# Expert stage of a mixture-of-experts block: single-buffered activations and a longer row of split weights

## The chip, the cores and the metric

One Trainium2 chip, and one of its cores. The metric is the device time of one execution of the whole kernel, in microseconds (us). The engines are called by their names in the profile: PE (TensorE matmul), DVE (VectorE), ACT (ScalarE), POOL (GpSimd) and SP (SyncE, which here only issues transfers).

## The reference, cut to what matters

The program is one block of a diffusion model on 2048 tokens of 1024 channels, all in fp32: a mixer layer, and then a layer of 16 experts. Only the second one is touched:

```python
def ec_moe(h, w_router, w_gate_e, w_up_e, w_down_e):
    cap = EC_CAPACITY * l // N_EXPERTS                      # 256 tokens for each of 16 experts
    aff = jax.nn.softmax((h @ w_router).astype(jnp.float32), axis=-1)
    top_aff, top_idx = lax.top_k(jnp.swapaxes(aff, 1, 2), cap)
    def per_set(hs, idx, wgt):
        xs = hs[idx]
        a = jax.nn.silu(jnp.einsum('ecd,edf->ecf', xs, w_gate_e)) * jnp.einsum('ecd,edf->ecf', xs, w_up_e)
        y = jnp.einsum('ecf,efd->ecd', a, w_down_e) * wgt[..., None].astype(hs.dtype)
        return jnp.zeros_like(hs).at[idx.reshape(-1)].add(y.reshape(-1, hs.shape[-1]))
```

Each expert picks its own 256 tokens, gathers their rows, multiplies them with three matrices of 1024 x 1024, and the weighted result is added to the rows it came from. A final RMS norm over all rows follows.

## The kernel before, in words

**Three products for one.** Every fp32 factor is split into a high and a low part in the type fp32r, and `mm3` (L252 to L255) adds three matmuls: high x high, low x high, high x low. A weight matrix comes in *units* of 128 x 1024 fp32 (512 KB). The class `Units` (L60) handles each in three steps: SP loads it into a tile `wraw` (L69), ACT copies it to `whi` (L78), and `wlo` = `wraw` - `whi` is made by DVE or POOL (L85). There are three buffers of each of the three tiles. A `wraw` is free for the next load once `wlo` is made; a pair `whi`, `wlo` is free once PE has used it. `c` counts the units used up, `s` those split, `d` those whose load is issued; `ahead(n)` splits up to `n` units as long as `s < c + nsp`, with `nsp` = 3, and keeps `nraw` = 3 loads issued beyond `s`. Who makes `wlo` is set by `low2`, since `LOWS` holds all four remainders: POOL from the top-k part through expert 0, DVE after that; `low` is not read in this stage.

**An expert has 12 items of 2 units.** `Flow.item` (L156) writes one item in this order: its 48 matmuls; the finish of the item before it; one step of every side generator; `ahead`, which here splits two units. Eight items `gate_up` (L1790) make `a` in eight pieces: ACT sigmoid (L1801), two DVE multiplications (L1802, L1803), ACT writes the high part `ah` (L1804) and DVE the low part `al` (L1805). Four items `down` (L1809) multiply `ah`, `al` with the down matrix, and DVE writes `y` (L1825). Before the first `down` the last piece's finish is written by `fl.flush()`; that piece is read by the last eighth of the item's matmuls (`LATE`, L45).

**The next expert is prepared beside it.** `prep(e + 1)` (L1726) is a side generator that starts with expert `e`: DVE writes a one-hot tile `oh` in two steps of eight (L1731), PE turns it into token numbers (L1737, 32 small matmuls), POOL gathers the rows into `xg0`, `xg1` (L1748), PE transposes them (L1766), and ACT and DVE split the result into `xh`, `xl` (L1771, L1772).

**Ahead of expert 0** stands the top-k search of experts 0 and 1 (`topk_first`, L1681): eight rounds, each a DVE count over a tile (L1684), a matmul, and a few tiny DVE instructions on integers (L1672, L1677, L1678, L1666), one after the other. `prep(0)` follows. One `next()` of that chain is one pass of the loop at L1893; in its first pass `un.ahead()` splits three units, their low parts on POOL. The search for experts 2 to 15 (`topk_rest`) has its eight rounds (DVE count at L1714, L1718, matmul at L1719) between the items of expert 0.

**The last six experts** (`LASTK`) carry more side work: rows of the output that are finished are loaded, normed and stored (`norm_row`, L1836), and each expert's result is added to gathered rows, normed and scattered (L1859 to L1888).

Of the kernel before, what the change touches and what calls it, by code (L numbers as in the profile page):

```python
# [11 lines left out]
F32R = mybir.dt.float32r  # L12
BF = mybir.dt.bfloat16
# [7 lines left out]
D = 1024  # L21
# [5 lines left out]
NSC = L // 128  # L27
# [32 lines left out]
class Units:  # L60
    def __init__(self, nc, pool, srcs, nraw, nsp, rset):
        self.nc, self.pool, self.srcs, self.nraw, self.nsp = nc, pool, srcs, nraw, nsp
        self.raw, self.hl, self.rset = {}, {}, rset
        self.d = self.s = self.c = 0
        self.low = self.low2 = nc.vector

    def _dma(self):
        raw = self.pool.tile([128, 1024], F32, name="wraw", bufs=self.nraw)
# [4 lines left out]
    def _split(self):  # L73
        if self.d == self.s:
            self._dma()
        raw = self.raw.pop(self.s)
        hi = self.pool.tile([128, 1024], F32R, name="whi", bufs=self.nsp)
        self.nc.scalar.activation(hi, raw, AF.Copy)  # L78
        if self.s in self.rset:
            lo = None  # L80
            v = lambda t: t.rearrange("p (k c) -> p k c", c=128)[:, :, 96:128]
            self.nc.vector.tensor_sub(v(hi), v(raw), v(hi).bitcast(F32))
        else:
            lo = self.pool.tile([128, 1024], F32R, name="wlo", bufs=self.nsp)
            (self.low2 if self.s % 4 in LOWS else self.low).tensor_sub(lo, raw, hi.bitcast(F32))  # L85
        self.hl[self.s] = (hi, lo)
        self.s += 1

    def loads(self, n=None):
        while self.d < min(len(self.srcs), self.s + self.nraw if n is None else n):  # L90
            self._dma()
# [138 lines left out]
def build(ctx, tc, A, out, dbg=None):  # L230
# [18 lines left out]

    RT, RG = Ring(ps_t, 2), Ring(ps_g, 4)  # L250

# [30 lines left out]
    un = Units(nc, wp, p1_units + p2_units * NBLK + p2_units[8:] + moe_units, 3, 3, rset)  # L282
# [120 lines left out]
    with tc.tile_pool(name="ada", bufs=1, side="right") as ada:  # L403
# [108 lines left out]
        for i in range(4):  # L512
            p = ps_a()
            for j in range(4):
# [24 lines left out]
                if hl and todo:  # L539
                    n = todo.pop(0)  # L540
# [19 lines left out]
    def x_first():  # L560
# [4 lines left out]
        yield  # L565
        for pr, R, bks in ((0, RG, (0, 1, 2, 3)), (1, RT, (0, 1)), (1, RG, (2, 3))):
            *ps, t = yield from R.get(len(bks))
# [21 lines left out]
    def gla_head(b, h, n, kd, qd, rt, vv, full, done=None, past=None, vdone=None):  # L589
        nch, nsc = n // 64, n // 128  # L590
        hs = slice(h * 128, (h + 1) * 128)
        v3 = lambda t: t.rearrange("p (s i) -> p s i", i=128)
        pz, tz = yield from RG.get()
        PE.matmul(pz[:, :n], wd[:, hs], rt[:, :n], start=True, stop=True)
# [6 lines left out]
        V.tensor_scalar(mz[:, :n], pz[:, :n], bd, 0.0, op0=OP.add, op1=OP.min)  # L601
        RG.put(tz)
        S.activation(zt[:, :n], zt[:, :n], AF.Exp, scale=-1.0)
# [58 lines left out]
        if full:  # L662
            pf, pb, tf = yield from RG.get(2)
            for s in range(4):
# [866 lines left out]
    for bi, b in enumerate(order):  # L1531
# [30 lines left out]
        xg = p2.tile([128, 4, D], F32, name="xg")  # L1562
# [26 lines left out]
    mo = moc.enter_context(tc.tile_pool(name="mo", bufs=1))  # L1589
# [7 lines left out]
        return psum.tile([128, 512], F32, name="pT", bufs=3)  # L1597

    RG = Ring(ps_g, 2)
    gt2 = mo.tile([128, D], F32)  # L1600
    fng = mo.tile([128, D], F32)
    brow(gt2, bc_d[0:1, 3072:4096])
# [123 lines left out]
    def prep(e, res):  # L1726
        while e not in ready:
            yield
        oh = mo.tile([128, NSC, 256], BF, name="oh", bufs=2)
        for t in range(NSC):  # L1730
            V.tensor_scalar(oh[:, t], iob, slot[:, e, t:t + 1], None, op0=OP.is_equal)  # L1731
            if t % 8 == 7:
                yield
        pa, tg = yield from RG.get()
        for t in range(NSC):
            for hf in range(2):
                PE.matmul(pa[:, hf * 5:hf * 5 + 5], oh[:, t, hf * 128:(hf + 1) * 128], aux[:, e, t],  # L1737
                          start=t + hf == 0, stop=t + hf == NSC)
        yield
        ax = mo.tile([128, 2, 5], F32, name="ax", bufs=2)  # L1740
        V.tensor_copy(ax.rearrange("p a b -> p (a b)"), pa[:, 0:10])
        RG.put(tg)
        idx, xg = [], []
        for i in range(2):
            ix = mo.tile([128, 1], I32, name=f"ix{i}", bufs=3)
            V.scalar_tensor_tensor(ix, ax[:, i, 0:1], 128.0, ax[:, i, 1:2], op0=OP.mult, op1=OP.add)
            x = mo.tile([128, D], F32R, name=f"xg{i}", bufs=2)
            G.indirect_dma_start(out=x.bitcast(F32), out_offset=None, in_=h2_d[:, :],  # L1748
                                 in_offset=bass.IndirectOffsetOnAxis(ap=ix[:, :1], axis=0))
            idx.append(ix)  # L1750
            xg.append(x)
        wt = mo.tile([128, 2], F32, name="wt", bufs=3)
        V.tensor_add(wt, ax[:, :, 2], ax[:, :, 3])
        V.tensor_add(wt, wt, ax[:, :, 4])
        if e == 0:
            for _ in range(PRE):
                next(rest)
        yield
        yield
        xh = mo.tile([128, KC, 256], F32R, name="xh", bufs=2)  # L1760
        xl = mo.tile([128, KC, 256], F32R, name="xl", bufs=2)
        def trans(p, bk, i):
            for k2 in range(2):
                kc = bk * 2 + k2
                o = (k2 * 2 + i) * 128
                PE.transpose(p[:, o:o + 128].bitcast(F32R), xg[i][:, kc * 128:(kc + 1) * 128], identr)  # L1766

        def evac(p, bk):
            p3 = p.rearrange("p (k t) -> p k t", k=2)
            ks = slice(bk * 2, bk * 2 + 2)  # L1770
            S.activation(xh[:, ks], p3, AF.Copy)  # L1771
            V.tensor_sub(xl[:, ks], p3, xh[:, ks].bitcast(F32))  # L1772

        if e == 0:
            ps = [ps_t(), ps_t(), ps_t(), ps_a()]
            for i in range(2):
                for bk in range(4):
                    trans(ps[bk], bk, i)
            for bk in range(4):
                evac(ps[bk], bk)  # L1780
        else:
            for bk in range(4):
                p = ps_t()
                for i in range(2):
                    trans(p, bk, i)
                yield
                evac(p, bk)
        res[e] = (xh, xl, idx, wt)
# [103 lines left out]
    un.low = un.low2 = G  # L1892
    for n, _ in enumerate(chain(topk_first(), prep(0, res))):  # L1893
        next(keys, None)
        if n == 0:
            un.ahead()
            un.low = V
    for e in range(E):
        special = e >= E - LASTK
        xh, xl, idx, wt = res.pop(e)  # L1900
        ah = mo.tile([128, 8, 256], F32R, name="ah", bufs=2)
        al = mo.tile([128, 8, 256], F32R, name="al", bufs=2)
        if e + 1 < E:
            fl.add(prep(e + 1, res))
        un.low2 = G if e == 0 else V
        if e == 0:
            fl.early.append(rest)
            fl.add(chain(delay(AD), split_aff(slice(HEAD_N, E), E - HEAD_N)))
        acs = []
        if special:  # L1910
            fl.add(acc_gather(idx, acs))
        if e == E - LASTK:
            fl.add(chain(delay(2), staggered([lambda t=t: norm_row(t) for t in range(NSC)], 4)))
        for f in range(8):
            gate_up(f, xh, xl, ah, al)
        y = [mo.tile([128, D], F32, name=f"y{i}", bufs=2) for i in range(2)]

        ss4 = mo.tile([128, 2, 4], F32, name="ss4", bufs=2)

        def fin_cols(j, i, e=e, y=y, acs=acs, ss4=ss4, idx=idx):  # L1920
            cs = slice(j * 256, (j + 1) * 256)
            V.tensor_add(y[i][:, cs], y[i][:, cs], acs[i][:, cs])
            if j < 2 or e < E - 1:
                fl.add(fin_late(j, i, e, y, acs, ss4, cs))
                return
            for _ in fin_late(j, i, e, y, acs, ss4, cs):
                pass
            if j == 3 and e == E - 1:
                for _ in final_row(i, e, y, acs, ss4, idx):
                    pass  # L1930

        def scat(e=e, y=y, idx=idx, special=special, ss4=ss4, acs=acs):
            if special and e < E - 1:
                fl.add(chain(delay(1), staggered([lambda i=i: final_row(i, e, y, acs, ss4, idx) for i in range(2)], 1)))
            elif not special:
                for i in range(2):
                    G.indirect_dma_start(out=x1_d[:, :],
                                         out_offset=bass.IndirectOffsetOnAxis(ap=idx[i][:, :1], axis=0),
                                         in_=y[i], in_offset=None, compute_op=OP.add)
        fl.flush()  # L1940
        for j in range(4):
            down(j, ah, al, y, wt, fin_cols if special else None, scat if j == 3 else None,
                 e == E - 1 and j == 3)
        fl.flush()
        if e == E - 1:
            fl.drain()
# [75 lines left out]
```

## Time and profile before

| | us |
|---|---|
| runs of the kernel, median of 3 | 2662.35 |
| lowest and highest of the 3 | 2653.22 and 2670.72 |
| span of the profiled execution, first to last instruction | 2667.8 |

The profiled execution's own time is not listed apart from its span; its span lies between the median and the highest run. In the span PE is busy for 2517.5 us (94%), DVE for 1881.2, ACT for 1252.5, POOL for 659.1. About 1440 us pass up to the end of the mixer's last product; some 40 us of top-k search and `prep(0)` follow, and the rest of the span belongs to the 16 experts.

### The profile page before, as it was taken

How to read it: one execution, taken by the hardware profiler on the slowest of the kernel's cores; microseconds unless marked ns; L12 is line 12 of the kernel's file. 1: busy time of each engine (PE TensorE's matmuls, PEld its weight loads, DVE VectorE, ACT ScalarE, POOL GpSimd, SP SyncE). 2: the span in 40 equal slices, each digit the busy share in tenths (PEclk: the TensorE clock that was granted, in tenths of full speed). 3: DMA queues.
4: the chain of work that ended last, by engine and by line, in shares of the span. 5: the costliest groups of instructions: out<-in, count | busy, mean ns of one | idle time of the engine just before them, and what ended most of it. 6: DMA issues, size and time to landing. Idle time of an engine off the chain costs nothing. (4 is left out here: it accounts for less than half of the span.)

```text
span 2667.8 us, 44973 instructions
## 1 busy us (share of the span) xinstructions
PE 2517.5 (94%) x17575; PEld 2295.5 (86%) x17575; DVE 1881.2 (71%) x3049; ACT 1252.5 (47%) x2128; POOL 659.1 (25%) x607
## 2 busy tenths in 40 slices
PE   7999999999998989999996899999999999999997
PEld 4878887887887768897886789999999999999997
DVE  6676668478368767767676866666666667778775
ACT  5454444344453345455553334444444445555553
POOL 0032157055225202131312550000000002323222
PEclk9999999999999989999997899999999999999999
DMA  7354356456435766656664356666666667787775
GB/s 259 125 188 164 137 186 220 144 174 213 161 112 170 251 225 221 222 185 225 199 210 139 127 174 212 215 204 209 212 207 214 211 209 251 262 276 258 252 248 183
DMA packets 202141, 537.00 MB, mean 201 GB/s; under 512 B 20871, under 2 KB 60216, under 8 KB 201928
## 3 DMA queue, kind: packets, MB, share of 16 engines
q1 hardware_dynamic: 141224, 408.77, 45.2%
q0 software_dynamic: 18592, 67.64, 8.8%
q10 hardware_dynamic: 42112, 57.72, 6.0%
q8 instruction: 138, 2.26, 0.3%
q14 instruction: 75, 0.61, 0.1%
HBM read 441.76 MB, written 92.29 MB: 200 GB/s over the span
## 5 line engine op out<-in xcount | busy, mean ns | idle before, releaser
L85 DVE TENSOR_TENSOR wlo<-wraw,whi 128x1024 fp32r<-128x1024 f32 x563 | 723.6, 1293 | 414.8 <-ACT whi L78 389.7
L78 ACT ACTIVATE whi<-wraw 128x1024 fp32r<-128x1024 f32 x595 | 623.8, 1055 | 619.7 <-PE pA L254 246.7
L255 PE MATMUL pA<-xh,wlo 128*128 128x256 f32 x2048 | 579.9, 283 | 17.3 <-DVE wlo L85 13.4
L253 PE MATMUL pA<-xh,whi 128*128 128x256 f32 x2048 | 582.1, 284 | 2.1 <-ACT whi L78 2.1
L254 PE MATMUL pA<-xl,whi 128*128 128x256 f32 x2048 | 577.4, 282 | 0.1
L255 PEld LDWEIGHTS pA<-xh,wlo 128*128 128x128 f32 x2048 | 388.0, 189 | 22.0 <-DVE wlo L85 17.4
L253 PEld LDWEIGHTS pA<-xh,whi 128*128 128x128 f32 x2048 | 388.0, 189 | 3.3 <-ACT whi L78 3.1
L254 PEld LDWEIGHTS pA<-xl,whi 128*128 128x128 f32 x2048 | 388.0, 189 | 0.4 <-DVE xl L1772 0.4
L253 PE MATMUL pA<-hh,whi 128*128 128x512 f32 (+1 forms) x912 | 366.4, 402 | 10.9 <-DVE kd L770 3.7
L255 PE MATMUL pA<-hh,wlo 128*128 128x512 f32 (+1 forms) x912 | 359.3, 394 | 0.4 <-DVE wlo L85 0.4
L254 PE MATMUL pA<-hl,whi 128*128 128x512 f32 (+1 forms) x912 | 359.1, 394 | 0.0
L253 PE MATMUL pA<-whi,ah 128*128 128x256 f32 x1024 | 290.3, 284 | 5.0 <-ACT ah L1804 5.0
L254 PE MATMUL pA<-wlo,ah 128*128 128x256 f32 x1024 | 287.4, 281 | 1.8 <-POOL wlo L85 1.1
L255 PE MATMUL pA<-whi,al 128*128 128x256 f32 x1024 | 287.8, 281 | 0.2 <-DVE al L1805 0.2
L253 PEld LDWEIGHTS pA<-hh,whi 128*128 128x128 f32 x912 | 175.4, 192 | 54.2 <-issue 8.9
L255 PEld LDWEIGHTS pA<-hh,wlo 128*128 128x128 f32 x912 | 174.9, 192 | 38.1 <-DVE wlo L85 0.7
L254 PEld LDWEIGHTS pA<-hl,whi 128*128 128x128 f32 x912 | 175.5, 192 | 34.3
L253 PEld LDWEIGHTS pA<-whi,ah 128*128 128x128 f32 x1024 | 193.7, 189 | 5.8 <-ACT ah L1804 5.8
L254 PEld LDWEIGHTS pA<-wlo,ah 128*128 128x128 f32 x1024 | 193.9, 189 | 2.6 <-POOL wlo L85 1.3
L255 PEld LDWEIGHTS pA<-whi,al 128*128 128x128 f32 x1024 | 193.7, 189 | 1.0 <-DVE al L1805 1.0
L1804 ACT ACTIVATE ah<-sg 128x256 fp32r<-128x256 f32 x128 | 53.5, 418 | 275.6 <-DVE sg L1803 275.6
L297 POOL TENSOR_TENSOR rs<-ms,neg_half 128x1 f32<-128x1 f32 (+2 forms) x70 | 54.5, 779 | 509.1 <-DVE ms L295 496.0
(438 smaller groups left out, 4787.7 us busy)
## 6 DMA issues: line engine op xcount, KB each, us to landing
wraw<-win SPq DMA_DIRECT2D x139, 512.0 KB
wraw<-wg SPq DMA_DIRECT2D x128, 512.0 KB
wraw<-wu SPq DMA_DIRECT2D x128, 512.0 KB
wraw<-wdn SPq DMA_DIRECT2D x128, 512.0 KB
wraw<-wout SPq DMA_DIRECT2D x40, 512.0 KB
ar<-ada SPq DMA_DIRECT2D x64, 256.0 KB
gate_d<-stg ACTq DMA_DIRECT2D x64, 256.0 KB
wraw<-wpj SPq DMA_DIRECT2D x32, 512.0 KB
```

Source lines behind the costliest of these rows:

```text
L78: self.nc.scalar.activation(hi, raw, AF.Copy)
L85: (self.low2 if self.s % 4 in LOWS else self.low).tensor_sub(lo, raw, hi.bitcast(F32))
L253: PE.matmul(ps, lh, rh, start=first, stop=False)
L254: PE.matmul(ps, lh, rl, start=False, stop=False)
L255: PE.matmul(ps, ll, rh, start=False, stop=last)
L297: G.tensor_tensor(r[:, :n], ms[:, :n], neg_half[:, :n], op=OP.pow)
L1804: S.activation(ah[:, f], sg, AF.Copy)
```

## The change

Three groups of tiles lose their second buffer: `ah` and `al` (8 KB of each partition each), `xg0` and `xg1` (4 KB each), `oh` (8 KB). The 32 KB hold four more pairs `whi`, `wlo`, which are taken from the stage's own pool `mo`; with the three of the pool `wp` they make seven. `nsp` becomes 7 when the stage begins (`widen`), and units go round through four buffers of the one and three of the other pool. The number of `wraw` buffers stays three. The loop over the search and `prep(0)` splits one unit in each pass, for seven passes, where it split three in the first pass.

```diff
+    def widen(self, pool, n):
+        self.more, self.nm, self.nsp = pool, n, self.nsp + n
+        self.k = 0
+
+    def _out(self, name):
+        if self.more is None:
+            return self.pool.tile([128, 1024], F32R, name=name, bufs=self.nsp)
+        if self.k % self.nsp < self.nm:
+            return self.more.tile([128, 1024], F32R, name=name + "m", bufs=self.nm)
+        return self.pool.tile([128, 1024], F32R, name=name, bufs=self.nsp - self.nm)
...
-        hi = self.pool.tile([128, 1024], F32R, name="whi", bufs=self.nsp)
+        hi = self._out("whi")
...
-            lo = self.pool.tile([128, 1024], F32R, name="wlo", bufs=self.nsp)
+            lo = self._out("wlo")
...
+        if self.more is not None:
+            self.k += 1
...
     RG = Ring(ps_g, 2)
+    un.widen(mo, 4)
...
-        oh = mo.tile([128, NSC, 256], BF, name="oh", bufs=2)
+        oh = mo.tile([128, NSC, 256], BF, name="oh")
...
-            x = mo.tile([128, D], F32R, name=f"xg{i}", bufs=2)
+            x = mo.tile([128, D], F32R, name=f"xg{i}")
...
     for n, _ in enumerate(chain(topk_first(), prep(0, res))):
         next(keys, None)
-        if n == 0:
-            un.ahead()
+        un.ahead(1)
+        if un.s == un.c + un.nsp:
             un.low = V
...
-        ah = mo.tile([128, 8, 256], F32R, name="ah", bufs=2)
-        al = mo.tile([128, 8, 256], F32R, name="al", bufs=2)
+        ah = mo.tile([128, 8, 256], F32R, name="ah")
+        al = mo.tile([128, 8, 256], F32R, name="al")
```

## Rows read from the trace of the kernel before

**Rows 1.** Timeline, PE, one-hot matmuls of three experts: start us, us, engine, line, instruction.
```profile
1657.60 0.96 PE L1737 MATMUL pG<-aux,oh 128*128 128x5 bf16 x32
...
2219.53 0.63 PE L1737 MATMUL pG<-aux,oh 128*128 128x5 bf16 x19
...
2519.23 0.91 PE L1737 MATMUL pG<-aux,oh 128*128 128x5 bf16 x30
```

**Rows 2.** Waits, PE, 1480 to 1600 us: who for whom, us in total, times, longest.
```profile
PE pG L1719 <- DVE mv L1718: 4.7, 2, 2.4
PE pA L255 <- POOL wlo L85: 3.9, 3, 3.0
...
PE pA L255 <- DVE wlo L85: 1.8, 2, 1.3
```

**Rows 3.** Waits, PE, 1600 us to the end.
```profile
PE pA L255 <- DVE wlo L85: 11.6, 13, 2.3
PE pA L253 <- ACT ah L1804: 5.0, 4, 2.1
```

**Rows 4.** Waits, ACT, 2348 to 2425 us (about expert 12).
```profile
ACT whi L78 <- DMA wraw<-wdn: 7.7, 3, 4.5
...
ACT whi L78 <- PE pA L254: 0.5, 1, 0.5
```

**Rows 5.** Waits, DVE, the same stretch, its longest.
```profile
DVE wlo L85 <- ACT whi L78: 11.7, 13, 2.2
```

**Rows 6.** Timeline, ACT then PE, 2401 to 2405 us; in brackets idle before, and what ended it.
```profile
2401.13 1.06 ACT L78 ACTIVATE whi<-wraw 128x1024 fp32r<-128x1024 f32 x1 [2.38 <-DMA wraw<-wdn]
...
2404.44 0.42 ACT L1804 ACTIVATE ah<-sg 128x256 fp32r<-128x256 f32 x1 [0.94 <-DVE sg L1803]
...
2404.91 0.39 PE L253 MATMUL pA<-whi,ah 128*128 128x256 f32 x1 [1.55 <-ACT ah L1804]
```

**Rows 7.** The chain of waits, 2366 to 2445 us, one load: start us, us.
```profile
2394.25 6.78 DMA wraw<-wdn
```

**Rows 8.** Timeline, POOL, DVE and SP, 1445 to 1455 us, search rounds of experts 0 and 1.
```profile
1446.23 6.95 POOL L85 TENSOR_TENSOR wlo<-wraw,whi 128x1024 fp32r<-128x1024 f32 x3 [3.94 <-ACT whi L78]
...
1445.01 0.16 DVE L1677 SCALAR_TENSOR_TENSOR cand<-dg,pj 128x1 int32<-128x1 int32 x1
...
1446.92 1.68 DVE L1677 SCALAR_TENSOR_TENSOR cand<-dg,pj 128x1 int32<-128x1 int32 x1
...
1449.31 1.59 DVE L1666 TENSOR_TENSOR pj<-P,jx 128x1 int32<-128x1 int32 x1
...
1451.04 2.15 DVE L1677 SCALAR_TENSOR_TENSOR cand<-dg,pj 128x1 int32<-128x1 int32 x1
...
1454.94 0.16 DVE L1677 SCALAR_TENSOR_TENSOR cand<-dg,pj 128x1 int32<-128x1 int32 x1
...
1448.61 0.33 SPq L69 DMA_DIRECT2D wraw<-wu  x1
```

**Rows 9.** Timeline, PE and DVE, 1511 to 1519 us, in expert 0.
```profile
1513.36 0.58 PE L255 MATMUL pA<-xh,wlo 128*128 128x256 f32 x1 [3.03 <-POOL wlo L85]
...
1511.38 4.27 DVE L1666 TENSOR_TENSOR pj<-P,jx 128x1 int32<-128x1 int32 x1
...
1518.69 0.17 DVE L1672 SCALAR_TENSOR_TENSOR m<-pG,mk 128x8 f32<-128x8 f32 x1 [1.20 <-PE pG L1719]
```

**Rows 10.** Timeline, ACT, DVE and POOL, 1694 to 1733 us, between two experts.
```profile
1694.81 0.58 ACT L1771 ACTIVATE xh<-pT 128x512 fp32r<-128x512 f32 x1
...
1719.65 0.42 ACT L1804 ACTIVATE ah<-sg 128x256 fp32r<-128x256 f32 x1 [1.81 <-DVE sg L1803]
...
1713.19 0.87 DVE L1825 SCALAR_TENSOR_TENSOR y<-pA,wt,gt 128x256 f32<-128x256 f32 x2
1713.98 1.74 DVE L1731 TENSOR_SCALAR oh<-iob,slot 128x256 bf16<-128x256 bf16 x8
...
1732.99 0.99 POOL L1748 DMA_INDIRECT xg<-h_d,ix  x1 [8.32 <-DVE wt L1754]
```

More of the change, by code (lines that the diff above doesn't have):

```diff
@@ L65, in __init__ @@
         self.low = self.low2 = nc.vector
+        self.more, self.nm = None, 0
+    def widen(self, pool, n):
[7 more added lines that the diff above has]
+        return self.pool.tile([128, 1024], F32R, name=name, bufs=self.nsp - self.nm)
     def _dma(self):
```

## The prediction

> **What bounds the kernel now.** I read the rows in the order of the stage's parts, since each has another limit. First the rhythm of the stage: one expert's one-hot matmuls follow the last expert's by the length of one expert [rows 1]. Between 1657.60 and 2219.53 us lie eight experts, so 70.24 us each; the three waits of PE that lead its list after 1600 us are nearly all in the last part, so in this middle part PE is the bound, and nothing that the change does to weights can make it faster. From 2219.53 to 2519.23 us four experts take 74.93 us each: 4.7 us lost per expert. Second, PE's waits [rows 2, 3]. In experts 0 and 1 they are for the search of experts 2 to 15 (4.7 us), for a low part from POOL (3.9 us) and for one from DVE (1.8 us). After 1600 us they are for `wlo` from DVE (11.6 us in 13 waits) and for `ah` at the turn from gate/up to down (5.0 us in 4). By these sums the last six experts seem to be short of weights in store, and a longer row of split units seems the remedy.
>
> Third, the question that decides: who waits for whom in those experts? Around expert 12 ACT waits 7.7 us for loads of down weights alone, and for PE 0.5 us in all; DVE's list holds only ACT [rows 4, 5]. So there PE is not what sets the pace. ACT and DVE go through their own instructions, in written order, as fast as the loads and their own work let them, and PE follows. The reader is to see this once in one place: ACT's copy at 2401.13 us waited 2.38 us for a load; behind it in ACT's order stands the last piece of `ah`, written at 2404.44 us, and PE had stood 1.55 us for it by 2404.91 us [rows 6]. Between issue and landing of such a load lie 6.78 us [rows 7].
>
> **The change, part by part.** The sum is made against the profiled execution, whose span of 2667.8 us is 5.4 us above the median of the runs shown; I carry the differences over to the median.
>
> *One buffer for `ah`, `al`, `oh`, `xg`.* Costs nothing, as the second buffer is not in use before. At the turn to the next expert the last `y` is evicted at 1713.19 us, so every reader of the old `ah` is done; the first write to the new one comes at 1719.65 us, 6.5 us later [rows 10]. The one-hots of 1713.98 us stand 56 us behind the matmuls that read the ones before (1657.60 us) [rows 1, 10], and the gather of 1732.99 us 38 us behind the evacuation (1694.81 us) of the rows gathered before [rows 10]. What hides it is the order in which the work is written; with that cover gone the wait would stand on ACT, DVE or POOL ahead of the splits.
>
> *Four more splits in the search.* SP gets four more loads there, ACT four more copies (1.06 us each [rows 6]), POOL four more subtractions. ACT's share is covered: the search runs on DVE and PE. SP has nothing urgent behind these loads, and the gather on POOL comes after the search. POOL's share is not covered. Three subtractions run from 1446.23 us for 6.95 us, 2.32 us each. In these 7 us three tiny integer instructions of DVE take 1.68, 1.59 and 2.15 us, where their like takes 0.16 before and after [rows 8]. The search's rounds show the price: from 1445.01 to 1446.92 us 1.91 us, and then 4.12 and 3.90 us (to 1451.04 and 1454.94), so 4.2 us for three, 1.4 us per subtraction. When do the new four run? The load of the fourth unit is issued at 1448.61 us, when the first subtraction gives its buffer back [rows 8]; with 6.78 us for a load [rows 7] and 1.06 us for the copy it can be subtracted from 1456.5 us on, and the others follow at 2.3 us or more. At 1454.94 us the fifth of eight rounds begins, and slots and one-hots follow, so all four fall among DVE work that PE idles for. 4 x 1.4 = +5.6 us. Bounds: 0, if they meet only instructions that POOL doesn't hold up; 9.3 us, if each holds DVE up for its whole length. I take the middle row, since it is the same work in the same loop.
>
> The Trainium skill ("SBUF — State Buffer", "Who interferes with whom") has a rule against this part: VectorE with two inputs from SBUF, or in a two-port mode, and GpSimd share a pair of ports, and the second to come is blocked until the first is through. The trace agrees with the 2.15 us beside 0.16; by the rule at its worst, a whole POOL instruction for each, this term would be the upper bound above.
>
> *Expert 0.* Here POOL still makes the low parts, two for each item as before. A store of four units more takes away PE's 3.9 us of waiting for POOL [rows 2], but PE also runs the search's matmuls between the items, and these wait for DVE. At 1513.36 us PE had stood 3.03 us for a low part; in the same time DVE sat in one integer instruction for 4.27 us, from 1511.38 us, and when it came to the next round it waited only 1.20 us for PE [rows 9]. What PE gains beyond that is waited off at the search. I take -1.2 us; bounds 0 and -3.9.
>
> *Expert 1.* DVE is relieved of the search, PE's 1.8 us of waiting for DVE's low parts goes [rows 2], and 680 us of PE-bound work lie behind it in which ACT and DVE catch up: -1.8 us; bounds 0 and that.
>
> *Experts 2 to 9.* Nothing: PE is the bound.
>
> *The last experts.* With seven pairs PE doesn't wait for `wlo` any more: the 11.6 us [rows 3] go from that line. What is late next is `ah`. The order of ACT's and DVE's instructions is not changed: in each item they still split two units, behind the same loads through the same three `wraw` buffers, and the last piece of `ah` still stands behind the last split of its expert. Since they hardly wait for PE, they reach that piece at the same time as before, and PE, earlier there by what it saved, waits there for as much longer. Once per expert the store is of no use. What can be gained is what ACT and DVE themselves wait for PE: 0.5 us [rows 4] for each of five experts, -2.5 us. Bounds: 0, and -19 us if the saved waits stay saved (below).
>
> Sum: +5.6 - 1.2 - 1.8 - 2.5 = +0.1 us, so 2662 us.
>
> **The rivals.**
> *Faster: the store carries over the turn.* ACT and DVE would have to catch up between a shortage and the next `ah`. For it: the shortages are short (13 waits, the longest 2.3 us), and expert by expert the loss is only 4.7 us. Against it: rows 4 and 5. Price: four experts lose 4 x 4.7 = 18.8 us up to 2519.23 us, and the remaining 1.7 another 8, together 27; the share of `wlo` in the waits for `wlo` and `ah` is 11.6 / 16.6, so 19 us. +5.6 - 1.2 - 1.8 - 19 = -16: 2646 us. Chance 0.22.
>
> *Slower: POOL holds up the search.* Place: the lead-in of expert 0. The price per subtraction is its whole 2.32 us instead of 1.4, since the slots and one-hots are closer packed than the rounds, and nothing comes back in expert 0 or at the end: +9.3 - 1.8 = +7.5, 2670 us. It decides from (1.2 + 1.8 + 2.5) / 4 = 1.4 us per subtraction on: that is just the price measured, so the sign of my sum is open. Chance 0.2.
>
> *Much slower: the single buffers bind.* If each expert's first piece kept PE waiting for its finish (1.81 + 0.42 us [rows 10]), 15 x 2.2 = 33 us: 2695 us. The Trainium skill ("Trainium Kernel Development and Optimization", "Best Practices") asks for double buffers so that transfers overlap compute; no row here shows the second buffer in use. Chance 0.03.
>
> *The store stays empty*, because loads come too slowly to fill it in the search: then the added cost and the gain both shrink, and the time is the forecast's. I count it with the forecast.
>
> **How the numbers follow.** Forecast 0.52, faster 0.22, slower 0.2, single buffers 0.03; 0.03 for what I don't see. The runs before differ by 17 us, so a median of three can be off by several us. The range takes in the faster case at 2646 less 4 and the slower one at 2670 plus 5: 2642 to 2675; the forecast's own is 2656 to 2668. A difference of 1% (26.6 us, about what a measurement of this kernel can tell from no change) needs a time under 2636 or over 2689: 0.07 for the first, the faster case with the expert 0 bound on top; 0.05 for the second, single buffers and the unseen; 0.88 between.
>
> **What would show it.** Right: PE's first `gate_up` of expert 0 begins 4 to 8 us later, with long integer instructions of DVE beside seven POOL subtractions; after 1600 us PE's waits for `wlo` are near zero and those for `ah` rise from 5.0 to 12 us or more; the last experts still take 74 to 75 us each. Wrong: `ah` waits stay at 5 us while `wlo` waits go, and the last experts come near 71 us (faster case); or the search isn't longer, which makes the time about 2657 us; or PE stands at the first items of each expert (single buffers).

## The result and the profile after

The changed kernel takes 2678.95 us (median of 7 runs, 2673.68 to 2682.94), the one before 2663.94 us on the same chip (7 runs): the ratio is 1.0061, with an interval of 1.0043 to 1.008. It is 15 us slower, where 2662 us and no change were forecast, and it lies above the range.

The profiled execution of after has a span of 2671.7 us and is the fastest of its seven, while that of before lies above its median. So the spans differ by only 3.9 us. But the first count of the search, ahead of which the two kernels do the same work, comes 4.9 us earlier in the profile of after (1436.46 against 1441.40 us). From that count to the end it is 1235.2 us for 1226.4: 8.8 us more. I compare stage by stage.

The rhythm, in the timeline of PE in the kernel after (start us, us, instruction; the same three experts as [rows 1]):
```profile
1658.98 0.96 PE L1752 MATMUL pG<-aux,oh 128*128 128x5 bf16 x32
...
2224.78 0.96 PE L1752 MATMUL pG<-aux,oh 128*128 128x5 bf16 x32
...
2525.51 0.96 PE L1752 MATMUL pG<-aux,oh 128*128 128x5 bf16 x32
```
Eight middle experts now take 565.80 us where it was 561.93 us [rows 1]: 70.73 us each for 70.24. The next four take 300.73 us for 299.70, and from there to the end it is 146.2 us for 148.6.

The lead-in, in the timeline of POOL and DVE in the kernel after (in brackets the idle time before, and what ended it), as [rows 8]:
```profile
1441.28 9.38 POOL L97 TENSOR_TENSOR wlom<-wraw,whim 128x1024 fp32r<-128x1024 f32 x4 [3.94 <-ACT whim L90]
1450.62 2.35 POOL L97 TENSOR_TENSOR wlo<-wraw,whi 128x1024 fp32r<-128x1024 f32 x1
1457.02 4.65 POOL L97 TENSOR_TENSOR wlo<-wraw,whi 128x1024 fp32r<-128x1024 f32 x2 [4.05 <-ACT whi L90]
...
1436.46 0.73 DVE L1699 TENSOR_SCALAR_CACHE_REDUCE tjk<-key,jx 128x512 bf16<-128x512 f32 x1
...
1441.99 1.65 DVE L1692 SCALAR_TENSOR_TENSOR cand<-dg,pj 128x1 int32<-128x1 int32 x1
...
1444.35 1.60 DVE L1681 TENSOR_TENSOR pj<-P,jx 128x1 int32<-128x1 int32 x1
...
1446.10 2.15 DVE L1692 SCALAR_TENSOR_TENSOR cand<-dg,pj 128x1 int32<-128x1 int32 x1
...
1448.96 1.72 DVE L1681 TENSOR_TENSOR pj<-P,jx 128x1 int32<-128x1 int32 x1
...
1450.82 2.16 DVE L1692 SCALAR_TENSOR_TENSOR cand<-dg,pj 128x1 int32<-128x1 int32 x1
...
1458.55 0.83 DVE L1693 SCALAR_TENSOR_TENSOR P<-dg,P 128x1 int32<-128x1 int32 x1
...
1460.14 1.58 DVE L1645 TENSOR_TENSOR msk<-aff,t 128x32 bf16<-128x32 f32 x1
...
1476.05 1.89 DVE L1787 TENSOR_TENSOR xl<-pT,xh 128x512 fp32r<-128x512 f32 x3 [5.19 <-ACT xh L1786]
```
Seven subtractions, and beside each of them one small DVE instruction that is held: three `cand`, two `pj`, a `P` and a `msk`, 0.83 to 2.16 us where 0.15 to 0.20 us is usual. Each ends within 0.1 us of the end of its subtraction. Together they take 10.6 us more than usual; the three of before [rows 8] took 5.0 us more. From the first count to the first `xl` it is 39.59 us; before it was 35.42 us (1441.40 to 1476.82). From there to the one-hot matmuls in the third expert (the first of [rows 1]) it is 182.93 us for 180.78.

Waits of PE in the kernel after (who for whom, us in total, times, longest), from 1480 to 1600 us, as [rows 2], and from 1600 us to the end, as [rows 3]:
```profile
PE pG L1734 <- DVE mv L1733: 11.8, 4, 4.4
PE pA L269 <- DVE al L1820: 1.7, 1, 1.7
...
PE pT L1781 <- DMA xg<-h_d,ix: 12.0, 7, 3.3
PE pA L267 <- ACT ah L1819: 6.3, 5, 2.6
```
Not one wait for a weight is left. In experts 0 and 1 PE waits for the search (`mv`) in their place. In the last experts it waits for the gathered rows `xg`, 12.0 us, and for `ah`, 6.3 us: 18.3 us in all, where five kinds of wait (the two of [rows 3] the largest) made 19.8 us before.

One such wait, in the timeline of PE and POOL:
```profile
2469.64 0.33 PE L1781 MATMUL pT<-identr,xg 128*128 128x128 f32 x2 [3.31 <-DMA xg<-h_d,ix]
...
2462.11 1.86 POOL L1763 DMA_INDIRECT xg<-h_d,ix  x1 [0.19 <-issue]
```
PE has the weights and comes to the transposes 3.31 us before the rows that POOL asked for at 2462.11 us are there. The indices for this gather are written by DVE, 8.86 us behind the one-hot matmuls of the same expert (2457.06 against 2448.20 us); before it was 4.94 us (2447.84 against 2442.90).

Waits of ACT in the kernel after, 2273 to 2600 us, those for loads (as in [rows 4], here for all the last experts):
```profile
ACT whim L90 <- DMA wraw<-wg: 18.8, 10, 3.6
ACT whim L90 <- DMA wraw<-wu: 11.0, 5, 3.9
ACT whi L90 <- DMA wraw<-wg: 10.8, 5, 4.0
ACT whi L90 <- DMA wraw<-wu: 5.4, 3, 2.7
ACT whim L90 <- DMA wraw<-wdn: 5.0, 4, 1.6
...
ACT whi L90 <- DMA wraw<-wdn: 4.0, 4, 1.3
```
Together 55.0 us in 31 waits; in the same stretch of before they are 47.1 us in 28. Four more pairs did nothing for the waits that hold ACT's order up.

### The profile page after: what moved, and what is told of

Read it like the earlier page. It is cut to its first block, busy times and chain, and to the rows that moved or that the text cites. A ratio compares the mean times of both kernels' runs of the same rounds, so it can differ in the third digit from the quotient of the medians.

```text
span 2671.7 us, 45172 instructions
## 1 busy us (share of the span) xinstructions
PE 2514.9 (94%) x17575; PEld 2298.7 (86%) x17575; DVE 1885.2 (71%) x3045; ACT 1252.7 (47%) x2128; POOL 675.1 (25%) x611
## 5 line engine op out<-in xcount | busy, mean ns | idle before, releaser
L97 DVE TENSOR_TENSOR wlo<-wraw,whi 128x1024 fp32r<-128x1024 f32 x358 | 461.1, 1293 | 277.2 <-ACT whi L90 264.8
L90 ACT ACTIVATE whi<-wraw 128x1024 fp32r<-128x1024 f32 x375 | 393.8, 1055 | 423.8 <-PE pA L268 226.4
L97 DVE TENSOR_TENSOR wlom<-wraw,whim 128x1024 fp32r<-128x1024 f32 x201 | 257.4, 1287 | 135.2 <-ACT whim L90 131.4
L267 PE MATMUL pA<-xh,whim 128*128 128x256 f32 x1176 | 335.5, 285 | 0.0
L268 PE MATMUL pA<-xl,whim 128*128 128x256 f32 x1176 | 333.0, 283 | 0.1
L269 PE MATMUL pA<-xh,wlom 128*128 128x256 f32 x1176 | 332.8, 283 | 0.0
L90 ACT ACTIVATE whim<-wraw 128x1024 fp32r<-128x1024 f32 x220 | 230.6, 1055 | 191.8 <-PE pA L269 68.6
L267 PE MATMUL pA<-xh,whi 128*128 128x256 f32 x872 | 248.5, 285 | 0.0
L268 PE MATMUL pA<-xl,whi 128*128 128x256 f32 x872 | 246.5, 283 | 0.0
L269 PE MATMUL pA<-xh,wlo 128*128 128x256 f32 x872 | 246.4, 283 | 0.0
```

Source lines behind the costliest of these rows:

```text
L267: PE.matmul(ps, lh, rh, start=first, stop=False)
L268: PE.matmul(ps, lh, rl, start=False, stop=False)
L269: PE.matmul(ps, ll, rh, start=False, stop=last)
```

## The experiments

Each ratio is against runs of the kernel before on the same chip, with its interval; medians of different experiments can come from different chips. "Middle experts" is the mean of eight from the one-hot matmuls of one expert to those eight later, as in [rows 1].

**1. One part alone: the single buffers** (before, with the four `bufs=2` of the diff removed, the freed memory left empty).

> The kernel before with single buffers for ah, al, oh and the gathered rows; three pairs of split weights and the lead-in stay as before, the freed memory is unused. Theory A (single buffers cost nothing; the loss is made of the lead-in, of slower matmuls on the new weight tiles, and of gains that turn into waits elsewhere): ratio 1.000 within 0.003, 70.2 us per expert in the middle part, PE's wait for gathered rows in the last experts under 2 us as before. Rival S (single buffers bind: the gather waits for its one buffer): PE's wait for gathered rows 10 us or more, as in the changed kernel (12.0 us), ratio 1.003 to 1.006.

2663.95 us, ratio 1.0004 (0.9982 to 1.0026), 70.24 us per middle expert. The second buffers were not in use.

**2. The lead-in undone and the pairs filled later:**
```diff
-    un.widen(mo, 4)
...
-        un.ahead(1)
-        if un.s == un.c + un.nsp:
+        if n == 0:
+            un.ahead()
             un.low = V
...
+        if e == 1:
+            un.widen(mo, 4)
```

> The changed kernel, but with the lead-in of before (three pairs split in the search, all by POOL) and the four further pairs added only when expert 1 begins, split by DVE. Their tiles come to lie at the top of the stage's memory. Theory A: the 4 us in the lead-in go, and what experts 0 and 1 lost with them; the middle part is at 70.2 or at 70.8 us per expert according to where the tiles lie; ratio 1.000 to 1.004. Rival L (the lead-in is all of the loss): ratio 1.000 or below. Rival S (single buffers bind): ratio 1.006 as the changed kernel.

2666.68 us, ratio 1.0014 (0.9992 to 1.0037). First count to first `xl` 35.6 us again. But the step from expert 1's one-hots to expert 2's grew to 98.0 us (95.1 in the changed kernel, 93.3 before): filling the store costs there too. And the middle experts took 69.75 us, less than before. The pairs had been allocated later and so stood elsewhere in memory; nothing else in that stage had changed. That was the first sign of what I had missed.

**3. Three pairs only, all in the new memory** (`widen(mo, 3)` with `nsp` = 3, old lead-in).

> The changed kernel with three pairs of split weights instead of seven, and all three in the new memory where the changed kernel has its four; lead-in of before. Theory A, part on placement (matmuls that read the new tiles run slower, 0.55 us per expert with 4 of 7 units there): with all units there 0.9 to 1.0 us per expert, so 71.1 to 71.2 us per expert in the middle part, ratio 1.004 to 1.006. Rival D (the slower pace comes with the number of pairs, or from somewhere else): 70.2 us per expert, ratio 1.000.

2669.59 us, ratio 1.0022 (1.0 to 1.0044), 70.84 us per middle expert, less than the 71.1 us I expected. Number and rotation of the pairs are those of before, and the single buffers cost nothing (experiment 1); only the place is new, and PE is slower.

**4. The same memory for raw weights** (single buffers, three pairs, seven `wraw` tiles):
```diff
+        if self.k % self.nraw < self.nm:
+            raw = self.more.tile([128, 1024], F32, name="wrawm", bufs=self.nm)
+        else:
+            raw = self.pool.tile([128, 1024], F32, name="wraw", bufs=self.nraw - self.nm)
```

> The kernel before with single buffers, and 16 of the 32 KB used for four more tiles of raw weights instead: seven loads under way or landed, three pairs split. Theory A, part on the last experts (ACT and DVE are held up there by loads that are issued only when one of three raw buffers comes free): the last experts fall from 74.9 us towards 71 to 72.5 us each, ACT's waits for weight loads after 2273 us fall below 10 us, ratio 0.991 to 0.996. Rival W (DVE's and ACT's own work in written order is the bound, or the transfers are): 74 to 75 us each, ratio 0.998 to 1.001.

2645.28 us, ratio 0.9929 (0.9907 to 0.9951). The middle experts stay at 70.25 us, and the last steps are 71.0 to 71.9 us where it was 71.4 to 76.8. The longest waits of ACT in this kernel, 2273 to 2600 us, and PE's waits from 1600 us on:
```profile
ACT ah L1817 <- DVE sg L1816: 88.2, 37, 5.9
ACT whi L90 <- PE pA L267: 17.4, 11, 2.0
...
PE pA L267 <- DVE wlo L97: 3.0, 9, 0.8
```
ACT's list holds no more waits for weight loads; its copies wait for PE, and PE's own waits have come down to 3.0 us, so PE is the bound. That settles the last experts: they were held by loads issued too late through three `wraw` buffers.

**5, 6. The place of the pairs, and the lead-in, each alone** (the changed kernel with the four pairs in a pool opened behind `mo`; the changed kernel with `if n == 0: un.ahead(3)` in the lead-in).

> The changed kernel with one difference: its four extra pairs stand at the top of the memory (behind every other tile of the expert stage) instead of at its bottom; seven pairs, the seven low parts on POOL in the lead-in and everything else as changed. Theory (the matmuls' pace depends on where their operands stand): the nine middle experts fall from some 70.75 us each to 69.6 to 70.0, the fifteen in all by 12 to 16 us, so 2663 to 2667 us. Rival (the slower pace comes from seven pairs in rotation or from what the lead-in left behind): 2677 to 2681 us and 70.7 us an expert.

2668.15 us, ratio 1.0024 (1.0008 to 1.004), 69.75 us per middle expert: 10.8 us less by place alone.

> The changed kernel, but only three low parts on POOL in the lead-in, as in the kernel before; the other four units are split in expert 0's first item. Place and number of the pairs as changed. Theory: the first count to the first xl goes back from 39.6 us to 35.5 (4 us less), the burst of four splits in expert 0 gives 0 to 3 us of that back, and the middle experts stay at 70.75: 2675 to 2680 us. Rival (the lead-in on POOL is most of the loss, through what it delays behind it): 2664 to 2668 us.

2680.41 us, ratio 1.0072 (1.0049 to 1.0096). The lead-in is back at 34.7 us (1440.08 to 1474.80), but the step from expert 0's one-hots to expert 1's went from 34.5 to 43.1 us. I had expected 0 to 3 us there. Written all at once into expert 0's first item, the four extra splits cost more (8.6 us) than spread over the lead-in (4.9 us).

**7, 8. Raw tiles and two more pairs; three pairs at the top** (the third experiment with the other pool).

> Single buffers, seven raw-weight tiles (four of them in the freed memory) and five pairs (two of them at the top of memory); three low parts on POOL in the lead-in, the other two splits in expert 0's first item. Theory (the last six experts are held by ScalarE's waits for late loads, more pairs give nothing, the place of the pairs some tenths of a us an expert): the last five steps near 71.5 us as with seven raw tiles alone, 2638 to 2646 us. Rival (pairs are worth something once the loads are early, PE then runs free in the last experts too): under 2636 us.

2639.59 us, ratio 0.9913 (0.9891 to 0.9935), 69.8 us per middle expert. The four steps up to the last one-hots are 69.7, 70.9, 70.4 and 73.6 us: no better than with seven raw tiles and three pairs.

> Three pairs only, all of them at the top of the memory of the expert stage; single buffers, lead-in as before. It is the run with three pairs at the bottom of the new memory (2669.6 us, 70.85 us an expert) with the place alone changed. Theory (place): 69.3 to 69.8 us per middle expert, 2650 to 2660 us. Rival (place among the new tiles is nothing; any tile outside the old pool is slower): 70.8 us an expert and 2668 to 2671 us.

2652.65 us, ratio 0.9967 (0.995 to 0.9984), 69.16 us per middle expert against 70.84 in the third experiment.

**9, 10. All pairs at the top, the six old tiles as raw tiles, with three and four pairs.**

> Three pairs, all at the top of the freed memory, and nine raw-weight tiles: the old three and the six tiles of the old pairs, which are free now. Single buffers, lead-in as before. Theory (the place is worth 1.1 us an expert against the kernel before, early loads some 17 us in the last experts, and the two add): the middle experts at 69.2 us, the last steps 70 to 72 us, 2626 to 2634 us. Rival (the six old tiles as targets of the loads disturb something, or the two gains overlap): 2638 us or more.

2630.46 us, ratio 0.9882 (0.9863 to 0.99), the fastest kernel of this study with the last one below. The two gains add.

> As the run with three pairs and nine raw tiles, with a fourth pair at the top; its first split stands in expert 0's first item. Theory (more pairs are worth nothing once the loads are early, each costs 1 to 2 us to fill at the start): 0 to 3 us above the run with three pairs. Rival (a fourth pair takes the rest of PE's waits in the last experts): 3 to 6 us below it.

2639.32 us, ratio 0.9909 (0.9889 to 0.9929): 9 us worse by the medians (4.4 us by the two profiled spans), more than I expected of a fourth pair. In its profile PE waits 15.3 us for gathered rows in the last experts, where the run with three pairs has 3.7 us.

**11. Seven pairs, but only three ahead in the last experts:**
```diff
-        while n and self.s < len(self.srcs) and self.s < self.c + self.nsp:
+        while n and self.s < len(self.srcs) and self.s < self.c + min(self.nsp, self.cap):
...
+        if e == E - LASTK:
+            un.cap = 3
```

> The changed kernel, but from the first of the last six experts on units are split no further ahead than three, as before; lead-in, buffers and place as changed. Theory (the last experts are set by the order of work on ScalarE and VectorE and their waits for late loads, and how far ahead the splits run only decides which wait shows): TensorE's waits for gathered rows in that stretch fall from 12.0 us to under 3 and waits for wlo come back to some 9 to 12 us, the steps stay at 72 to 78 us, 2675 to 2683 us. Rival (running seven ahead is worth several us there, the gain was only hidden by the slower matmuls): 2685 us or more.

2667.18 us, ratio 1.002 (1.0006 to 1.0034): faster than the changed kernel, which neither theory allowed. PE's waits in this kernel, 2265 us to the end, the longest three:
```profile
PE pA L269 <- DVE wlom L97: 5.3, 7, 1.4
PE pA L269 <- DVE wlo L97: 3.6, 3, 2.1
PE pA L267 <- ACT ah L1819: 3.1, 4, 1.2
```
The waits for gathered rows are gone and weight waits are back, as expected: in experts 12 to 15 DVE writes the indices 4.4 to 5.1 us behind the one-hot matmuls, where it is 6.9 to 8.9 us in the changed kernel. But the medians differ by 11.8 us, of which the two profiles show 4.0 (spans 2667.7 and 2671.7), behind the last one-hots. So running far ahead is of no use there and seems to cost. How much is not settled.

**12. The same three pairs one place lower** (behind `al`).

> The run with three pairs at the top, with the pairs one place lower: directly behind al, 31 KB of each partition below the top place, all tiles of x, ah and al where they were in that run. Theory (what counts is that the pairs stand behind the x and ah tiles and not in front of them): 69.1 to 69.3 us per middle expert, 2650 to 2656 us. Rival (the pace falls evenly with the address, from 70.85 us at 94 KB to 69.16 at 195 KB): 69.6 to 69.8 us per middle expert and 2658 to 2663 us.

2672.77 us, ratio 1.004 (1.0026 to 1.0054), 71.5 us per middle expert: the slowest place of all, and both theories wrong. It is neither "behind x" nor "high". One thing in which the three places, before and after do differ is the start of the pairs against the start of `x`, `xl`, `ah` and `al`, taken modulo 128 bytes of a partition. The compiled programs place `x` at 32 throughout; the pairs stand at 32 here (offset 0), at 64 in the kernel before (32), at 96 at the top (64), and at 0 in the third experiment and the changed kernel's four new pairs (96). The same matmuls at offset 0, in this kernel, PE, 1660 to 2150 us (in the line the count, busy us, mean ns) and in its timeline:
```profile
L267 PE MATMUL pA<-xh,whim 128*128 128x256 f32 x871 | 247.9, 285 | 0.0
...
1720.09 0.28 PE L269 MATMUL pA<-xh,wlom 128*128 128x256 f32 x1
...
1720.69 0.28 PE L268 MATMUL pA<-xl,whim 128*128 128x256 f32 x1
```
and at offset 64, in the kernel with three pairs at the top:
```profile
L267 PE MATMUL pA<-xh,whim 128*128 128x256 f32 x915 | 255.8, 280 | 0.0
...
1720.09 0.28 PE L269 MATMUL pA<-xh,wlom 128*128 128x256 f32 x1
...
1720.66 0.28 PE L268 MATMUL pA<-xl,whim 128*128 128x256 f32 x1
```
Five starts later it is 0.60 us in the one and 0.57 us in the other. Neither line shows a wait. Over all neighbours less than 150 ns apart between 1660 and 2150 us the gate and up matmuls start every 120.0 ns at offset 0, 118.3 ns at 32 (before), 114.9 ns at 64 and 118.4 ns (third experiment) at 96. The down matmuls, where the weights are the 256 columns and `ah` or `al` is the operand of 128 x 128, start every 120.0, 116.9, 117.1 and 120.0 ns: 96 is as slow as 0 for them, while for gate and up it is no slower than 32.

That is where the changed kernel loses, since it has both places side by side. Its down matmuls on the four new pairs (`whim`, `wlom`, offset 96) and on the three old ones (`whi`, `wlo`, offset 32), PE, 1660 to 2150 us:
```profile
L267 PE MATMUL pA<-whim,ah 128*128 128x256 f32 x256 | 72.8, 284 | 0.0
...
L268 PE MATMUL pA<-wlom,ah 128*128 128x256 f32 x256 | 72.1, 282 | 0.0
L267 PE MATMUL pA<-whi,ah 128*128 128x256 f32 x192 | 54.1, 282 | 0.0
...
L268 PE MATMUL pA<-wlo,ah 128*128 128x256 f32 x192 | 53.6, 279 | 0.0
```
Start to start it is 119.9 ns on the new pairs and 117.0 on the old; for gate and up it is 119.0 and 118.3. For four sevenths of an expert's 192 down and 384 gate and up matmuls that makes 0.46 of the 0.48 us that a middle expert lost, and two thirds of it are the down matmuls'.

**13 to 16. The offset alone, by pads of 64 to 96 bytes.** The pads are tiles of 16, 16, 16 + 8 and 24 words, such as
```diff
+        if e == 0:
+            pad = mo.tile([128, 16], F32, name="pad")
+            G.memset(pad[:, 0:1], 0.0)
```

> The run with three pairs directly behind al (71.43 us per expert) with a pad of 64 bytes per partition between al and the pairs, nothing else. Theory (what counts is the offset of the pairs against x, xl, ah and al within 128 bytes; here it goes from 0 to 64): 69.0 to 69.4 us per middle expert, 2650 to 2658 us. Rival (the region of memory counts): still 71.4 us and 2670 to 2676 us.

2652.1 us, ratio 0.9955 (0.9938 to 0.9971), 69.28 us per middle expert. A pad of 64 bytes takes 20.7 us off.

> The run with three pairs at the top (69.16 us per expert) with a pad of 64 bytes per partition ahead of the pairs, so that their offset against x and ah within 128 bytes goes from 64 to 0. Theory (offset): 71.3 to 71.5 us per middle expert, 2668 to 2678 us. Rival (region): still 69.2 us and 2650 to 2656 us.

2672.17 us, ratio 1.0036 (1.0024 to 1.0048), 70.9 us. The fast place is slow at offset 0, if not quite as slow as the place below it (71.5).

> The changed kernel with 64 bytes of pad per partition ahead of the four new pairs and 32 bytes behind them; all seven pairs then stand 64 bytes off x, xl, ah and al within 128 bytes (the new four stood 96 off, the old three 32). Theory (offset): 69.0 to 69.4 us per middle expert where it was 70.75, so some 23 us less in fifteen experts: 2652 to 2660 us. Rival (region or number of pairs): 70.7 us and 2676 to 2682 us.

2662.51 us, ratio 1.0001 (0.999 to 1.0012), 68.96 us: 16.4 us less than the changed kernel, by 96 bytes, though 2.5 us above the range I expected.

> The kernel before with 96 bytes of pad per partition at the start of the expert stage's memory, so that x, xl, ah and al stand 64 bytes off the three pairs within 128 bytes where it was 32. Theory (offset): 69.0 to 69.4 us per middle expert where it was 70.24, 2644 to 2652 us. Rival: 70.2 us and 2660 to 2664 us.

2650.62 us, ratio 0.9953 (0.9939 to 0.9968), 68.99 us. The last two runs are before and after with the offset made equal, and so show the change without the accident of its place. PE's waits from 2200 us to the end, in the changed kernel with pads:
```profile
PE pA L267 <- ACT ah L1824: 15.2, 6, 4.1
PE pT L1786 <- DMA xg<-h_d,ix: 7.5, 6, 1.7
```
and in the kernel before with a pad:
```profile
PE pA L255 <- DVE wlo L85: 14.8, 14, 3.5
PE pA L253 <- ACT ah L1806: 4.8, 5, 1.5
PE pA L253 <- ACT whi L78: 1.5, 3, 0.5
PE pA L254 <- DVE wlo L85: 1.5, 5, 0.4
PE pT L1768 <- DMA xg<-h_d,ix: 0.5, 1, 0.5
```
22.7 us in the one and 23.1 us in the other. The saved waits came back almost whole, under other names.

**17, 18. The offset in the mixer, and everything together** (a constant tile of 64 bytes moved from ahead of the pairs to behind them).
```diff
-    sl = consts.tile([128, 16], F32)
...
     c1 = c1c.enter_context(tc.tile_pool(name="c1", bufs=1))
+    sl = c1.tile([128, 16], F32)
```

> The kernel before with one small constant tile of 64 bytes per partition moved from ahead of the weight pairs to behind them. The pairs move down by 64 bytes; against hh and hl of the mixer their offset within 128 bytes goes from 0 to 64, against yh, yl and ogh, ogl by sign alone, and against x and ah it stays as it was. Theory (offset): the mixer's matmuls on hh and hl with 256 columns fall from 121.8 ns start to start to some 117, those with 512 columns from 227.5 by 2 to 6, so 9 to 20 us less in all: 2642 to 2653 us; the experts stay at 70.24 us. Rival (the rule holds for the expert stage's tiles alone): 2659 to 2665 us.

2661.1 us, ratio 1.0 (0.9989 to 1.0011). Two groups of PE's instructions, up to 1440 us, in this kernel:
```profile
L253 PE MATMUL pA<-hh,whi 128*128 128x512 f32 x896 | 361.5, 404 | 11.0 <-DVE kd L770 3.7 <-ACT stg L776 3.5 <-DVE vv L760 1.3
...
L253 PE MATMUL pA<-whi,hh 128*128 128x256 f32 x288 | 80.6, 280 | 0.5 <-ACT whi L78 0.5
```
The matmuls with 256 columns got faster, as forecast: from 119.8 to 114.0 ns start to start for this group (82.4 us busy before). Those with 512 columns, where `hh` and `hl` have the 512 columns, got slower by 1.4 to 1.8 ns (227.7 to 229.2 in the mean of the groups) and there are three times as many, so some 5 us won and some 4 us lost. The rule doesn't carry over to them.

> Three pairs 64 bytes off x and ah, nine raw-weight tiles, single buffers (2630.5 us), and the small constant tile moved as in the other run. Theory: the two add, 2611 to 2622 us. Rival: 2627 to 2634 us.

2631.38 us, ratio 0.989 (0.9875 to 0.9906): the same as without the move. Both are 1.1 to 1.2% faster than before.

## Why the prediction was wrong, step by step

**Two steps failed.** The sum was to be +0.1 us. From the first count on, the profiles show +8.8 us: +4.2 in the lead-in, +2.2 in experts 0 and 1, +3.9 in the eight middle experts, +1.0 in the next four and -2.4 from there to the end. The medians are 15.0 us apart; the profiled run of after is the fastest of its seven, and where the other 6 us lie no trace shows.

**The first step that failed is "Experts 2 to 9. Nothing: PE is the bound."** PE is the bound there, and that was the reason to look at PE's own time. The change moves four of seven pairs to other addresses, and each expert takes 0.48 us longer, +3.9 us in eight, without one wait in the list. I had taken the duration of a matmul as given by its shape. Shown in two ways: in the changed kernel the same matmuls are slower on the new pairs than on the old (experiment 12), and 96 bytes of pads take 16.4 us off it (13 to 16). Why the offset matters to the chip is not shown.

**The second is experts 0 and 1** (-1.2 and -1.8 forecast). They had the wrong sign: +2.2 us up to the one-hot matmuls in the third expert, 5.2 us off and by the profiles the largest miss, and +4.5 us in the pair with equal offset (182.8 against 178.3). I had written that what PE gained beyond 1.2 us it would wait off at the search. It waited off more: `mv` rose from 4.7 us [rows 2] to 11.8 us, while the waits for low parts that went were 6.8 us (5.7 of them in [rows 2]); with equal offset it was 14.7 us against 5.5, for 7.0 us that went. Experiments 2 and 6 show that filling four more pairs costs several us wherever it is put. What makes it so dear in experts 0 and 1 stays open. The nine `mv` themselves take 11.4 us where they took 8.5, but they take 10.8 in the run with single buffers as well, where PE waits for them 4.7 us as before.

**The lead-in** (+5.6 forecast, bounds 0 to 9.3) was right in kind. It cost 4.2 us (39.59 against 35.42), and 4.5 us in the pair with equal offset (39.5 against 35.0). The held DVE instructions took 5.6 us more for four subtractions more, which is just the 1.4 us each that I had read off, but not all of it reached the end of the lead-in. When the four run I had wrong: the fourth load, issued at 1443.66 us, was copied from 1447.17 us on, 3.5 us later and not 6.78, so two of the four followed the first three at once. Nor is it the fifth round that begins behind 1454.94 us but the sixth. Neither changes the sum. The trace agrees with the Trainium skill ("SBUF — State Buffer", "Who interferes with whom") on DVE instructions that are blocked beside POOL until it is through: seven of them, each up to the end of its subtraction. None was held for a whole subtraction of 2.3 us, so the upper bound was not reached.

**The last experts** (-2.5 forecast, about -1.4 measured) were right in the main point, that weights in store turn into other waits because ACT and DVE set the pace. It is shown at equal offset: 22.7 us of waits against 23.1, and 301.6 us against 301.9 for the same four experts. I was wrong on where they would turn up. I named `ah`; in the changed kernel the larger part is the wait for gathered rows, whose indices DVE writes later when it splits further ahead, as experiment 11 shows. With the pads it is `ah` again (15.2 of 22.7 us). And the 0.5 us that ACT waits for PE [rows 4] was that of one expert; from 2273 to 2600 us the list of before has 7.3 us of it, so the -2.5 us rested on a stretch that was not typical. Behind the last one-hots the changed kernel with pads takes 148.5 us to its end, the other 146.8.

**The sum at equal offset**, from the two spans of 2657.4 and 2648.4 us: -1.2 us ahead of the first count, where nothing differs, +4.5 lead-in, +4.5 experts 0 and 1, -0.2 middle, -0.3 last four, +1.7 end: +9.0 us. The medians say 11.9. So by the medians most of the 15 us is not the place of the pairs: it lies in the lead-in and in experts 0 and 1. What is left for the place is 3 us by the medians and 7 by the pace (15 x 0.48); runs of this kernel scatter too much to say more.

**The rivals.** "Store carries over the turn" is refuted. "Single buffers bind" is refuted (1.0004). "POOL holds up the search" had the right sign and was right that nothing comes back in expert 0; but its price, 9.3 us for the lead-in, did not come (4.2), and its sum lacks both the loss in experts 0 and 1 and the slower matmuls. None of my rivals had PE itself slower.

## What to carry to other kernels

Before you give freed memory to a ring, find which ring is late: here ACT's waits for loads [rows 4] named the raw tiles, and half of the same 32 KB brought -0.7% there, where all of it brought +0.6% as split weights. An allocation moves everything behind it. Where PE is the bound, compare the start-to-start time of the same matmul before and after; if it moved with no wait beside it, try a small pad before you look for a cause in the schedule.

## What the runs showed of the hardware

The pace of a matmul with 128 x 256 fp32 operands depends on where its two operands start. By the offset of their start addresses modulo 128 bytes (0, 32, 64, 96) the gate and up matmuls start every 120.0, 118.3, 114.9 and 118.4 ns, the down matmuls every 120.0, 116.9, 117.1 and 120.0 ns; the granted clock was 1.00 (2.4 GHz) over the whole stretch at each. The offset is not all of the rule: at offset 0 by a pad at the top it is 118.8 and 119.4 ns, at offset 64 by a pad in the kernel before 116.1 and 114.8 ns, and for 512 columns offset 64 was no gain. The Trainium skill ("SBUF — State Buffer", "Who interferes with whom") says that only the port pair shared by VectorE and GpSimd causes contention, and that PE reads the moving operand and the weights through independent ports. That names nothing through which the pads could act; here they moved the time by 12 to 21 us, and the measurement decides. Whether it is contention at all is not shown.

While a subtraction of POOL ran, a small DVE instruction with two inputs from SBUF was held to its end: 0.83 to 2.16 us where 0.15 to 0.20 us is usual, seven times in the changed kernel's lead-in.
